# Starting the channel mixer's first product before its norm is known, in a two-layer decoder trunk on one core

## The chip, the cores and the metric

The kernel runs on one core of one Trainium2 chip, in one launch. Its time is device time in microseconds. Five engines work side by side, each through its own instructions in a fixed order: TensorE (PE in the profile, with its weight loads as PEld) multiplies, ScalarE (ACT) evaluates a function with a scale and a bias, VectorE (DVE) does elementwise work, GpSimd (POOL) here only raises to a power, and SyncE (SP) issues the loads. Engines meet at semaphores: an instruction waits until what it reads is written and what it overwrites has been read.

## What is computed

A trunk of two layers over 256 tokens of width 1024, all in float32. Each layer has a token mixer (three branches, gates, an output projection) and a channel mixer, each behind a norm whose shift and scale come from a conditioning vector c. The part that the change touches:

```python
def rms_norm(x, g):
    y = x * lax.rsqrt(jnp.mean(x * x, axis=-1, keepdims=True) + NORM_EPS)
    return y * g

def modulate(h, shift, scale):
    return h * (1.0 + scale[:, None, :]) + shift[:, None, :]

def channel_mixer(h, w_up, ffn_dw_w, ffn_dw_b, w_down):      # w_up: 1024 x 5632, w_down: 2816 x 1024
    u = causal_depthwise_conv(h @ w_up, ffn_dw_w, ffn_dw_b)  # 3 taps along the tokens
    a, b = jnp.split(u, 2, axis=-1)
    return (jax.nn.silu(a) * b) @ w_down

# in each layer, behind y = token_mixer(...) = merged @ w_out
x = x + g1[:, None, :] * y
h = modulate(rms_norm(x, ffn_norm_g[l]), sh2, sc2)
x = x + g2[:, None, :] * channel_mixer(h, w_up[l], ffn_dw_w[l], ffn_dw_b[l], w_down[l])
```

The norm's factor, called rstd below, is one number per token. So h @ w_up is rstd times (x * g * (1 + scale)) @ w_up, plus shift @ w_up, which is the same for all tokens.

## The kernel before

x lies transposed in SBUF, the on-chip memory: eight tiles of 128 features by 256 tokens (S). A product accumulates in PSUM, in banks of 512 float32 per partition, taken from two pools, psa and psb.

**Products.** Every float32 weight and every operand is split into a rounded high part and the low part that remains, and each product is three matmuls: high by high (L300), high weight by low operand (L301), low weight by high operand (L303). `mmw` queues products and `flush` issues them, all L303 behind all others; at the end of an accumulation it goes bank by bank instead (L294 to L296). A unit of weights is 128 x 1024, 512 KB: SP loads it into one of four `raw` buffers (L199), ACT writes its high part `whi` (L222), DVE its low part `wlo` (L224), which frees the buffer. `take` keeps some units split ahead of use; `issue_after` tells the scheduler to put an instruction behind another. The order on each engine is fixed when the program is built, by a scheduler that weighs these hints with estimates of its own.

**The boundary**, from the token mixer's projection to the channel mixer, lies in `layer` from L1249 on. `project(7)` ends the accumulation in four psa banks. Eight residuals (L1251) add it, times g1, to x. `norm_stats` then squares the eight tiles on ACT (L530), adds them in pairs on DVE (L540), and sums over the features in four pairs of one-column matmuls against a vector of ones (L545). DVE and POOL make rstd of that (L519, L520). `bcast_rows` spreads it over the partitions with a matmul against the identity (L555). Around these stand fourteen warm-up matmuls on a constant bf16 tile (L322, in groups of 4, 7 and 3 by `WARM1`), and filling steps: `mod_part(l, 5)` computes the last part of c's modulation, eight steps of four matmuls (L407) whose weights (`in_wm`) go through four spare buffers (`SPARE`). `norm_tile` makes the operand tile by tile: x times gain times rstd (L603, DVE), plus shift, rounded (L604, ACT), and the low part (L605, DVE). Then four small operations prepare the taps of the convolution.

**The channel mixer** runs 22 units up(j), each two weight units of four k-tiles with an a and a b half in one psb bank, and 22 units down(j), which accumulate in four psa banks. `FFN` orders them with `FLEAD` up units ahead of the downs. Behind up(j) come the taps on ACT (L1298) and DVE (L1300), silu and product, and the split of the result. In layer 0, the rows of layer 1's modulation (`in_wmr`, into spare buffers) fill DVE and SP.

## Time and profile before

| | us |
|---|---|
| three runs | 909.5, 912.25, 909.32 (median 909.5) |
| profiled execution | 909.82 |
| its span, first to last instruction | 907.7 |
| layer 0's boundary, projection's end to up(1)'s end | 271.13 to 291.76 |
| layer 1's boundary | 711.45 to 731.67 |
| layer 1's entry, sums of squares to broadcast's end | 464.62 to 469.04 |

The profile is of one execution. Its page gives busy times, the chain of work that ended last, and groups of instructions by line; the timeline lists each instruction with its start, and in brackets how long its engine had idled and who released it. A row such as `psa<-mhl,whi` names the output and the inputs by the program's names. The granted clock of TensorE (PEclk) is given as a share of full speed.

### The profile page before, as it was taken

The numbers are of one execution on the slowest core, as the hardware profiler recorded it, in microseconds if no ns is written. First come the engines' busy times: TensorE is split into PE (matmuls) and PEld (weight loads), VectorE is DVE, ScalarE is ACT, GpSimd is POOL, SyncE is SP. The second block draws the span as 40 slices with busy tenths as digits, with TensorE's granted clock in tenths as the row PEclk, the third lists the DMA queues.
The fourth block names the chain that finished last, engine by engine and source line by source line (L and its number), as shares of the span: only waits on it lengthen the run. The fifth ranks groups of instructions, "written<-read, shape, count | busy, mean of one in ns | idle before, by whom it ended". The sixth has DMA issues, their size and how long they took to land.

```text
span 907.7 us, 18736 instructions
## 1 busy us (share of the span) xinstructions
PE 888.3 (98%) x7339; PEld 841.5 (93%) x7339; DVE 797.1 (88%) x1554; ACT 555.2 (61%) x979; POOL 46.2 (5%) x36
## 2 busy tenths in 40 slices
PE   7999999999999999999999999999999999999998
PEld 6888888999998999999989988989999899999998
DVE  6989999999988999998764999999887798777774
ACT  4677588644755655556543676986475565565551
POOL 1010700000000000000000043000000000000000
PEclk9999999999999999999999999999999999999999
DMA  8956535699988889996633664157768676566631
GB/s 321 379 196 202 187 118 183 214 334 320 304 292 308 295 296 312 313 301 211 200 112 108 197 223 161 53 184 244 264 206 270 221 259 189 186 194 199 190 92 47
DMA packets 57976, 201.59 MB, mean 222 GB/s; under 512 B 6944, under 2 KB 8480, under 8 KB 57888
## 3 DMA queue, kind: packets, MB, share of 16 engines
q1 hardware_dynamic: 57888, 200.41, 66.6%
q8 instruction: 57, 0.93, 0.4%
q14 instruction: 31, 0.25, 0.1%
HBM read 199.33 MB, written 1.05 MB: 221 GB/s over the span
## 4 chain that ended last, share of the span: by engine, by line
PE 78%; DVE 12%; ACT 4%; DMA 3%; issue 2%; SPq 0%; POOL 0%; POOLq 0%; DVEq 0%; ACTq 0%
PE psb L300 16%; PE psb L301 16%; PE psb L303 15%; PE psa L300 7%; PE psa L301 7%; PE psa L303 7%; DVE wlo L224 3%; DVE cacc L1103 3%; PE psa L407 2%; DVE raw L778 1%; ACT whi L222 1%; PE psa L294 1%; DVE raw L390 1%; DMA raw<-in_win 1%; ACT p L675 1%
## 5 line engine op out<-in xcount | busy, mean ns | idle before, releaser
L222 ACT ACTIVATE whi<-raw 128x1024 fp32r<-128x1024 f32 (+2 forms) x286 | 296.6, 1043 | 217.6 <-PE psb L301 117.3
L224 DVE TENSOR_TENSOR wlo<-raw,whi 128x1024 fp32r<-128x1024 f32 (+2 forms) x286 | 340.3, 1195 | 65.5 <-ACT whi L222 57.9
L300 PE MATMUL psb<-hh,whi 128*128 128x256 f32 x1088 | 263.5, 282 | 0.5 <-ACT p L675 0.3
L301 PE MATMUL psb<-hl,whi 128*128 128x256 f32 x1088 | 261.0, 280 | 0.0
L300 PEld LDWEIGHTS psb<-hh,whi 128*128 128x128 f32 x1088 | 205.0, 189 | 6.3 <-issue 3.8
L301 PEld LDWEIGHTS psb<-hl,whi 128*128 128x128 f32 x1088 | 205.0, 189 | 0.5 <-DVE wlo L224 0.4
L303 PE MATMUL psb<-hh,wlo 128*128 128x256 f32 x1088 | 149.2, 279 | 0.0
L303 PEld LDWEIGHTS psb<-hh,wlo 128*128 128x128 f32 x1088 | 135.6, 188 | 0.8 <-issue 0.8
L1103 DVE SCALAR_TENSOR_TENSOR cacc<-upad,cw,cacc 128x256 f32<-128x256 f32 x240 | 105.7, 477 | 0.4
L300 PE MATMUL psa<-mhl,whi 128*128 128x256 f32 x400 | 94.0, 278 | 0.0
L301 PE MATMUL psa<-mhl,whi 128*128 128x256 f32 x400 | 93.7, 278 | 0.0
L1300 DVE SCALAR_TENSOR_TENSOR e<-psb,fw,e 128x255 f32<-128x255 f32 (+1 forms) x176 | 84.0, 477 | 5.4 <-ACT e L1298 4.5
L520 POOL TENSOR_TENSOR rs<-rs,mhalf 128x8 f32<-128x8 f32 (+3 forms) x26 | 44.6, 1729 | 669.2 <-DVE rs L519 669.1
L300 PEld LDWEIGHTS psa<-mhl,whi 128*128 128x128 f32 x400 | 75.0, 188 | 0.0
L301 PEld LDWEIGHTS psa<-mhl,whi 128*128 128x128 f32 x400 | 75.0, 188 | 0.0
L1298 ACT ACTIVATE e<-psb,fb,fw 128x256 f32<-128x256 f32 x88 | 48.5, 551 | 22.4 <-DVE e L1300 19.2
L390 DVE SCALAR_TENSOR_TENSOR raw<-raw,crow 128x1024 f32<-128x1024 f32 x48 | 58.5, 1218 | 0.5 <-DMA raw<-in_wmr 0.5
L303 PE MATMUL psa<-mhl,wlo 128*128 128x256 f32 x400 | 53.9, 277 | 0.0
L303 PEld LDWEIGHTS psa<-mhl,wlo 128*128 128x128 f32 x400 | 49.4, 188 | 0.0
L1308 ACT ACTIVATE mhl<-e 128x256 fp32r<-128x256 f32 x44 | 18.3, 416 | 30.1 <-DVE e L1306 27.6
L300 PE MATMUL psb<-whi,hh 128*128 128x416 f32 (+1 forms) x96 | 30.9, 350 | 4.5 <-ACT hh L854 4.5
L301 PE MATMUL psb<-whi,hl 128*128 128x416 f32 (+1 forms) x96 | 29.6, 343 | 0.2 <-DVE hl L855 0.2
(275 smaller groups left out, 1474.3 us busy)
## 6 DMA issues: line engine op xcount, KB each, us to landing
raw<-in_wup SPq DMA_DIRECT2D x88, 512.0 KB, 4.9
raw<-in_wmr SPq DMA_DIRECT2D x60, 512.0 KB, 5.7
raw<-in_wdn SPq DMA_DIRECT2D x44, 512.0 KB, 4.5
raw<-in_wm SPq DMA_DIRECT2D x32, 512.0 KB, 4.7
raw<-in_wgab SPq DMA_DIRECT2D x32, 512.0 KB, 4.9
raw<-in_wqkv SPq DMA_DIRECT2D x24, 512.0 KB, 5.1
raw<-in_win SPq DMA_DIRECT2D x16, 512.0 KB, 4.7
raw<-in_wgc SPq DMA_DIRECT2D x16, 512.0 KB, 4.3
```

What stands on the lines that cost most here:

```text
L222: ac.activation(hi, raw, AF.Copy)
L224: ve.tensor_tensor(lo, raw, hi.bitcast(F32), op=ALU.subtract)
L300: te.matmul(o, p1[0], p1[1], start=start, stop=False)
L301: te.matmul(o, p2[0], p2[1], start=False, stop=False)
L303: te.matmul(o, p3[0], p3[1], start=False, stop=stop)
L390: ve.scalar_tensor_tensor(raw, raw, scale, row, op0=ALU.mult, op1=ALU.mult, accum_out=acc)
L407: te.matmul(acc[32 * c:32 * c + 32, 0:S], cact[:, k:k + 1].to_broadcast([P, 32]), raw[:, c * S:(c + 1) * S], start=(k == 0), stop=(k == KD ...
L520: gp.tensor_tensor(r, r, mhalf[:, :n], op=ALU.pow)
L1103: ve.scalar_tensor_tensor(aj, upad[:, j, t:t + S], cw[:, j * 31 + t:j * 31 + t + 1], aj, op0=ALU.mult, op1=ALU.add)
L1298: ac.activation(t, src, AF.Identity, scale=fw[:, 2, c:c + 1], bias=fb[:, c:c + 1])
L1300: ve.scalar_tensor_tensor(t[:, d:S], src[:, 0:S - d], fw[:, 2 - d, c:c + 1], t[:, d:S], op0=ALU.mult, op1=ALU.add)
L1308: ac.activation(mh, th, AF.Copy)
```

## The change

Layer by layer, up(0) is taken apart from the other up units. Its operand becomes u = x * gain (without rstd and shift), split into high and low, and it starts as soon as the tiles of x are there. Two columns that hold the shift stand beside the 256 tokens of each operand tile, so that one matmul of 258 columns also gives shift @ w_up. The product stands in two psa banks (`pre`) and is multiplied by rstd, with the shift's column added, when it is read. The other up units still read the normalised tiles.

```diff
+    def raw_operand(sh):
+        parts = [operand([P, 4 * S], t, "u") for t in SPARE] + [
+            wk.tile([P, 4 * (S + 30)], F32R, tag="upad", name=nm("u"), bufs=1)]
...
+    def boundary(update, gs, sh, fill, part):
+        uh, ul = raw_operand(sh)
+        st = psb()
+        for n in range(KD):
+            update(n)
+            sq = e1()
+            ac.activation(sq, x[:, n, :], AF.Square)
+            if n % 2 == 0:
+                one = sq
+            else:
+                ve.tensor_tensor(one, one, sq, op=ALU.add)
+                if n < KD - 1:
+                    for b in range(NB):
+                        te.matmul(st[:, b:b + 1], one[:, b * P:(b + 1) * P], ones, start=(n == 1 and b == 0),
+                                  stop=False)
+            ac.activation(uh[n][:, 0:S], x[:, n, :], AF.Identity, scale=gs[:, n:n + 1])
+            ve.scalar_tensor_tensor(ul[n][:, 0:S], x[:, n, :], gs[:, n:n + 1], uh[n][:, 0:S].bitcast(F32),
+                                    op0=ALU.mult, op1=ALU.subtract)
+        mid = part(0, uh, ul)
+        with tc.issue_after(mid.ins):
+            for b in range(NB):
+                last = te.matmul(st[:, b:b + 1], one[:, b * P:(b + 1) * P], ones, start=False, stop=(b == 1))
+        r = rstd_of(st[:, 0:NB], NB, 1.0 / D)
+        with tc.issue_after(last.ins):
+            mid = part(1, uh, ul)
+        with tc.issue_after(mid.ins):
+            step(fill, 2)
+        with tc.issue_after(fills[-1].ins):
+            bc = bcast_rows(r)
+        with tc.issue_after(rows_last[0].ins):
+            step(fill, KD - 2)
+        return bc
...
+        def part0(part, uh, ul):
+            if part == 0:
+                pre.extend(psa() for _ in range(2))
+            behind[0] = 2
+            holds[:] = [rst[0].ins] if part else []
+            for k, w in take()[0]:
+                for i in range(2):
+                    mmw(pre[i][:, 0:S + 2], cut(w, i, P), (uh[k], ul[k]), k == 0, k == KD - 1)
+            return flush()
...
-        fill = mod_part(l, 5)
-        bc = norm_stats(fill)
+        fill = mod_part(l, 5, (("vb", 1), ("lh2", 1), ("lh0", 1), ("lh1", 1), ("qkT", 2), ("qkT", 2)))
+        bc = boundary(residual, gs2, mod[l][:, 24:32], fill, part0)
...
         def up(j):
-            pp = psb()
...
+            if j == 0:
+                bcs = e1()
+                ac.activation(bcs, bc, AF.Copy)
...
+                    ve.tensor_tensor(src, pre[i][:, 0:S], bcs, op=ALU.mult)
+                    cb = small(1, "m0", 4)
+                    ve.tensor_copy(cb, pre[i][:, S:S + 1])
+                    ac.activation(src, src, AF.Identity, bias=cb)
```

The order around it is changed too. The broadcast is a transpose in all norms, and no longer a float32 product; the warm-up matmuls of these two boundaries are gone (those of layer 1's entry stay). The filling weights have six buffers. `behind` lets `take` load units that it does not split yet, and `holds` names the instruction behind which the next low part is put:

```diff
-            rows_last[0] = te.matmul(bc[:, b * P:(b + 1) * P], r[:, b:b + 1].to_broadcast([P, P]), ident,
-                                     start=True, stop=True)
+            rows_last[0] = te.transpose(bc[:, b * P:(b + 1) * P], r[:, b:b + 1].to_broadcast([P, P]), ident)
...
-        while coming and len(ready) < n + ahead[0]:
+        while coming and len(ready) + len(raws_in) < n + ahead[0]:
             src, ks, lead = coming.pop()
-            ready.append((split(wload_unit(src), lead), src.shape[1] // len(ks), ks))
+            raws_in.append((wload_unit(src), lead, src.shape[1] // len(ks), ks))
+            while raws_in and len(ready) < n + ahead[0] - behind[0]:
+                raw, lead, c, ks = raws_in.pop(0)
+                ready.append((split(raw, lead), c, ks))
...
-FLEAD = 1
+FLEAD = 0
```

`behind` is 1 from project(6) on, 2 in up(0), and 0 behind it. The taps of the convolution are prepared earlier in the layer; the normalised tiles are each held behind the one two before; layer 1's tables (`prepare`, three kinds of small DVE operations) come to stand inside layer 0's boundary; `FLEAD` at 0 puts one more up unit ahead of down(0).

What the scheduler makes of it on PE, at layer 0's boundary, from the projection's end on. Before (psa_3532 is the filling accumulation, psb_3546 the sums of squares, psb_3589 the broadcast, psb_3671 up(0)):

```order
L407 MATMUL psa_3532<-raw_3533,cact 32x256 x4
L407 MATMUL psa_3532<-raw_3539,cact 32x256 x4
L545 MATMUL psb_3546<-ones,e_628_3547 128x1 x2
L545 MATMUL psb_3546<-ones,e_630_3554 128x1 x2
L322 LDWEIGHTS warm_w
L322 MATMUL psb_3545<-warm_w 128x256
...
L555 MATMUL psb_3589<-ident,rs_3586 128x128 x2
...
L407 MATMUL psa_3532<-raw_3595,cact 32x256 x4
L407 MATMUL psa_3532<-raw_3601,cact 32x256 x4
L407 MATMUL psa_3532<-raw_3607,cact 32x256 x4
L407 MATMUL psa_3532<-raw_3613,cact 32x256 x4
L300 MATMUL psb_3671<-hh_3631,whi_3376 128x256
```

After, from the low weights of up(0)'s first half (psa_3588 and psa_3589 are its two banks, psb_3537 the sums, psb_3664 the broadcast; the operand tiles u_3526 and u_3527 hold high parts, u_3529 low ones):

```order
L308 MATMUL psa_3588<-u_3527,wlo_3383 128x258
L308 MATMUL psa_3589<-u_3527,wlo_3383 128x258
L648 MATMUL psb_3537<-ones,e_633_3565 128x1 x2
L656 MATMUL psb_3537<-ones,e_635_3578 128x1 x2
L305 MATMUL psa_3588<-u_3527,whi_3462 128x258
L306 MATMUL psa_3588<-u_3529,whi_3462 128x258
...
L308 MATMUL psa_3589<-u_3530,wlo_3463 128x258
L413 MATMUL psa_3651<-raw_3652,cact 32x256 x4
L413 MATMUL psa_3651<-raw_3658,cact 32x256 x4
L560 MATMUL psb_3664<-ident,rs_3618 128x128 x2
L413 MATMUL psa_3651<-raw_3667,cact 32x256 x4
L413 MATMUL psa_3651<-raw_3673,cact 32x256 x4
```

Up(0) now stands ahead of the last sums and the broadcast, in two halves, and the filling steps stand behind it.

ACT in layer 0, from the projection's last operands (`mhl`, high part) to the first squares. Before:

```order
L222 ACTIVATE whi_3376<-raw_3374 128x1024
L1184 ACTIVATE mhl_3397<-e_604_3393 128x256
L1180 ACTIVATE e_609_3418<-psb_3405,col_146 128x256
L222 ACTIVATE whi_3456<-raw_3454 128x1024
L1184 ACTIVATE mhl_3422<-e_609_3418 128x256
L530 ACTIVATE e_628_3547<-x 128x256
L530 ACTIVATE e_629_3549<-x 128x256
L530 ACTIVATE e_630_3554<-x 128x256
L530 ACTIVATE e_631_3556<-x 128x256
```

After (raw_3590 is the second unit of up(1), the fourth up unit that SP loads; L641 are the squares, L650 the scaled x):

```order
L222 ACTIVATE whi_3382<-raw_3380 128x1024
L1245 ACTIVATE mhl_3403<-e_606_3399 128x256
L1241 ACTIVATE e_611_3424<-psb_3411,col_146 128x256
L222 ACTIVATE whi_3767<-raw_3590 128x1024
L222 ACTIVATE whi_3462<-raw_3460 128x1024
L1245 ACTIVATE mhl_3428<-e_611_3424 128x256
L641 ACTIVATE e_629_3539<-x 128x256
L650 ACTIVATE u_3526<-x,gs_3524 128x256
...
L650 ACTIVATE u_3527<-x,gs_3524 128x256
L222 ACTIVATE whi_3623<-raw_3466 128x1024
L222 ACTIVATE whi_3771<-raw_3621 128x1024
L641 ACTIVATE e_633_3565<-x 128x256
```

A split of raw_3590 has come between the two operands of the projection, and two splits stand between the fourth and the fifth tile.

ACT in layer 1, at the same place, after the change (raw_9431 is the fifth up unit that SP loads in this layer):

```order
L222 ACTIVATE whi_9224<-raw_9222 128x1024
L1245 ACTIVATE mhl_9210<-e_1569_9206 128x256
L222 ACTIVATE whi_9278<-raw_9276 128x1024
L222 ACTIVATE whi_9581<-raw_9431 128x1024
L641 ACTIVATE e_1590_9349<-x 128x256
L650 ACTIVATE u_9336<-x,gs_9334 128x256
...
L650 ACTIVATE u_9337<-x,gs_9334 128x256
L222 ACTIVATE whi_9433<-raw_9282 128x1024
L641 ACTIVATE e_1595_9380<-x 128x256
```

Here the added split stands behind the projection's last operand (mhl_9210) and right ahead of the first square, where before the squares followed the split of the unit loaded before it.

More of the change, by code (lines that the diff above doesn't have):

```diff
@@ L207, in trunk_kernel @@
     hold = [None]
+    holds = []
     raw_tags = [("raw", 4)]
@@ L222, in split @@
         ac.activation(hi, raw, AF.Copy)
-        with tc.issue_after(hold[0]) if hold[0] else ExitStack():
+        after = holds.pop(0) if holds else hold[0]
+        with tc.issue_after(after) if after else ExitStack():
             ve.tensor_tensor(lo, raw, hi.bitcast(F32), op=ALU.subtract)
@@ L302, in flush @@
         for o, _, _, p3, _, stop in queue:
-            te.matmul(o, p3[0], p3[1], start=False, stop=stop)
+            last = te.matmul(o, p3[0], p3[1], start=False, stop=stop)
         queue.clear()
+        return last
     def cut(w, i, n):
@@ L530, in sq_sums @@
             ac.activation(sq, src, AF.Square)
-            if alone and k >= n - 2:
-                one = sq
-            elif k % 2 == 0:
+            if k % 2 == 0:
                 if SQ4 and n == 4 and k:
@@ L542, in sq_sums @@
                     continue
-            with tc.issue_after(warm(bank, WARM1[0]).ins) if bank is not None and WARM1[0] and k == n - 2 + (not alone) else ExitStack():
+            with tc.issue_after(warm(bank, WARM1[0]).ins) if bank is not None and WARM1[0] and k == n - 1 else ExitStack():
                 for b in range(NB):
@@ L574, in norm_stats @@
             with tc.issue_after(last.ins):
-                step(fill, 3 if SHORT else KD - F1)
+                step(fill, KD - F1)
         return bc
@@ L606, in norm_tile, with ends @@
         return a, v
+    def raw_operand(sh):
+        uh, ul = [], []
+        parts = [operand([P, 4 * S], t, "u") for t in SPARE] + [
+            wk.tile([P, 4 * (S + 30)], F32R, tag="upad", name=nm("u"), bufs=1)]
+        for dst, (i0, i1), at in ((uh, (0, 1), 0), (ul, (2, 3), 2)):
+            for k in range(KD):
+                i, o = ((i0, i1, 4)[k // 3], k % 3 + (at if k > 5 else 0))
+                dst.append(parts[i][:, o * (S + 2):(o + 1) * (S + 2)])
+        for k0, k1 in ((0, 3), (3, 6), (6, 8)):
+            i, o = ((0, 1, 4)[k0 // 3], 0)
+            n = k1 - k0
+            def ends(i, o):
+                return parts[i][:, o * (S + 2):(o + n) * (S + 2)].rearrange("p (k c) -> p k c", k=n)[:, :, S:S + 2]
+            hi, lo = ends((0, 1, 4)[k0 // 3], 0), ends((2, 3, 4)[k0 // 3], 2 if k0 > 5 else 0)
+            src = sh[:, k0:k1].unsqueeze(2).to_broadcast([P, n, 2])
+            ac.activation(hi, src, AF.Copy)
+            ve.tensor_tensor(lo, src, hi.bitcast(F32), op=ALU.subtract)
+        return uh, ul
@@ L915, in layer @@
         upad = wk.tile([P, 4, S + 30], F32, tag="upad", name=nm("upad"), bufs=1)
-        ve.memset(upad[:, :, 0:30], 0.0)
+        with tc.issue_after(normed[0].ins) if l else ExitStack():
+            ve.memset(upad[:, :, 0:30], 0.0)
         def glu(j):
@@ L1267, in layer, with residual @@
             ve.tensor_scalar(fb[:, NF:44], cv(l, "fdw_b")[:, NF:44], 0.5, None, op0=ALU.mult)
+        for tok in CFG["order"][l]:
+            run[tok[0]](*tok[1:])
+            if tok == ("OC", 0):
+                taps()
+        step(mods, 99)
+        g1h = small(8, "g1h", 2)
+        ve.tensor_scalar(g1h, mod[l][:, 16:24], 0.5, None, op0=ALU.mult)
+        def residual(n):
+            ve.scalar_tensor_tensor(x[:, n, :], acc[n // 2][:, (n % 2) * S:(n % 2 + 1) * S], g1h[:, n:n + 1],
+                                    x[:, n, :], op0=ALU.mult, op1=ALU.add)
+        pre = []
+        def part0(part, uh, ul):
[7 more added lines that the diff above has]
+            return flush()
+        gs2 = mod_gain(l, 4, "ffn_g")
+        fill = mod_part(l, 5, (("vb", 1), ("lh2", 1), ("lh0", 1), ("lh1", 1), ("qkT", 2), ("qkT", 2)))
+        bc = boundary(residual, gs2, mod[l][:, 24:32], fill, part0)
+        hh, hl = new_h()
+        marks = []
+        for k in range(KD):
+            marks.append(norm_tile(k, bc, gs2[:, k:k + 1], mod[l][:, 24 + k:25 + k], hh, hl,
+                                   marks[k - 2] if k > 1 else None))
+        behind[0] = 0
         acc2 = []
@@ L1285, in up @@
         def up(j):
-            pp = psb()
-            for _ in range(2):
-                for k, w in take()[0]:
-                    for i in range(2):
-                        mmw(pp[:, i * S:(i + 1) * S], cut(w, i, P), (hh[:, k, :], hl[:, k, :]), k == 0 and i == 0,
-                            k == KD - 1 and i == 1)
-                flush()
+            if j == 0:
+                bcs = e1()
+                ac.activation(bcs, bc, AF.Copy)
+            else:
+                pp = psb()
+                for _ in range(2):
+                    for k, w in take()[0]:
+                        for i in range(2):
+                            mmw(pp[:, i * S:(i + 1) * S], cut(w, i, P), (hh[:, k, :], hl[:, k, :]), k == 0 and i == 0,
+                                k == KD - 1 and i == 1)
+                    flush()
             ab = []
```

58 lines of the change are left out of this document (26 added, 32 removed).

## Prediction

> **What bounds the kernel now.** First the head of the profile page: the span, the busy shares, and the engines of the chain of work that ended last.
>
> ```profile
> span 907.7 us, 18736 instructions
> PE 888.3 (98%) x7339; PEld 841.5 (93%) x7339; DVE 797.1 (88%) x1554; ACT 555.2 (61%) x979; POOL 46.2 (5%) x36
> PE 78%; DVE 12%; ACT 4%; DMA 3%; issue 2%; SPq 0%; POOL 0%; POOLq 0%; DVEq 0%; ACTq 0%
> ```
>
> TensorE (PE) is busy for 98% of the span, so the time falls only where PE does needless work or waits. The change works at the two boundaries between token mixer and channel mixer. PE's timeline at layer 0's boundary follows (start, duration, what ran; a row may hold several instructions, and a float32 product is recorded twice, so x16 at L407 is two steps of four).
>
> ```profile
> 271.13 1.07 PE L407 MATMUL psa<-raw,cact 128*32 128x256 f32 x16
> 272.13 1.05 PE L545 MATMUL psb<-ones,e 128*128 128x1 f32 x8
> 273.04 0.60 PE L322 MATMUL psb<-warm_w 128*128 128x256 bf16 x4
> 273.63 1.24 PE L545 MATMUL psb<-ones,e 128*128 128x1 f32 x8
> 274.74 0.92 PE L322 MATMUL psb<-warm_w 128*128 128x256 bf16 x7
> 275.97 0.71 PE L555 MATMUL psb<-ident,rs 128*128 128x128 f32 x4 [0.31 <-POOL rs L520]
> 276.52 0.49 PE L322 MATMUL psb<-warm_w 128*128 128x256 bf16 x3
> 276.94 1.93 PE L407 MATMUL psa<-raw,cact 128*32 128x256 f32 x32
> ...
> 281.19 0.64 PE L407 MATMUL psa<-raw,cact 128*32 128x256 f32 x8 [0.23 <-DMA raw<-in_wm]
> ...
> 290.86 1.07 PE L303 MATMUL psb<-hh,wlo 128*128 128x256 f32 x8
> 291.76 0.28 PE L300 MATMUL psb<-hh,whi 128*128 128x256 f32 x1
> 291.88 0.28 PE L301 MATMUL psb<-hl,whi 128*128 128x256 f32 x1
> ```
>
> The projection ends at 271.13, where the first filling step (L407) starts, and up(1) at 291.76: 20.6 us. Work that stays: up(0) and up(1), 96 matmuls at 0.1125 us (eight in the 0.90 from 290.86) to 0.12 (291.76 to 291.88), I take 0.116, 11.1 us; eight filling steps at 0.5 (two in the 1.00 from 271.13), 4.0; the sums of squares 0.91 and 1.11; the broadcast 0.55. Together 17.7, so **2.9 us are spare**: 14 warm-up matmuls (0.59, 0.92 and 0.42), the wait for rstd, 0.31, that for a load, 0.23, and short waits for normalised tiles. Layer 1:
>
> ```profile
> 711.45 1.07 PE L407 MATMUL psa<-raw,cact 128*32 128x256 f32 x16
> ...
> 730.77 1.07 PE L303 MATMUL psb<-hh,wlo 128*128 128x256 f32 x8
> ```
>
> From 711.45 to 731.67 (730.77 plus 0.90) are 20.2 us, 2.5 spare. **The ceiling at the two boundaries is 5.4 us, 0.6%**, if PE never waits there.
>
> **The change, part by part.** *The new chain that feeds PE.* PE begins up(0) without rstd, but needs its operand: for each of eight tiles ScalarE (ACT) makes a square and the rounded scaled x, VectorE (DVE) the residual and the remainder. ACT works in order:
>
> ```profile
> 264.40 1.07 ACT L222 ACTIVATE whi<-raw 128x1024 fp32r<-128x1024 f32 x1 [0.49 <-PE psa L301]
> 265.67 0.42 ACT L1184 ACTIVATE mhl<-e 128x256 fp32r<-128x256 f32 x1 [0.20 <-DVE e L1182]
> 271.46 1.01 ACT L530 ACTIVATE e<-x 128x256 f32<-128x256 f32 x3
> 290.11 0.57 ACT L1298 ACTIVATE e<-psb,fb,fw 128x256 f32<-128x256 f32 x1 [2.18 <-DVE e L1300]
> 290.57 0.41 ACT L1304 ACTIVATE e<-e 128x256 f32<-128x256 f32 x1
> ```
>
> A square costs 0.32 us (three in 1.01, less the overlap), an activation whose scale is a column, as that of scaled x is, 0.46 (290.11 to 290.57), a weight split 0.96 (1.07 less an overlap of 0.1). In layer 0 two splits stand between the fourth and the fifth tile: 8 x 0.78 + 2 x 0.96 = **8.2 us** from the first square to the last scaled tile, against 4.3 of PE's own (24 matmuls, three pairs of sums at 0.5). ACT is late here, not PE.
>
> *When this chain starts in layer 0.* In the new order ACT does one more split, of raw_3590, ahead of the high half of the projection's last operand (row 265.67 before). That unit is the fourth up unit that SP loads, issued at 261.4 in the trace of before:
>
> ```profile
> L199 SPq DMA_DIRECT2D raw<-in_wup x1: 328/328/328, 261.4 to 261.4; - x1
> DMA to landing us min/median/max: 5.4/5.4/5.4
> ```
>
> ```profile
> 265.11 0.28 PE L294 MATMUL psa<-mhl,whi 128*128 128x256 f32 x1
> 266.14 0.50 PE L294 MATMUL psa<-mhl,whi 128*128 128x256 f32 x2 [0.19 <-ACT mhl L1184]
> ```
>
> The load's issue hangs on a buffer whose release does not move, so it lands at 261.4 + 5.4 = 266.8 as before. ACT stands until then; two splits and the operand follow, to 266.8 + 1.92 + 0.3 = 269.0. PE, in its last flush of the projection since 265.11, has 11 matmuls (1.25 us) that don't need it, and stands from 266.4 to 269.0: **2.6 us**, where it waited 0.19 before. Sixteen matmuls later the first bank is whole; with drain and residual,
>
> ```profile
> 268.06 1.66 DVE L1251 SCALAR_TENSOR_TENSOR x<-psa,g1h,x 128x256 f32<-128x256 f32 x4 [0.95 <-PE psa L296]
> 271.64 1.22 DVE L224 TENSOR_TENSOR wlo<-raw,whi 128x1024 fp32r<-128x1024 f32 x1
> ```
>
> the first residual (268.06 before, 0.40 each) comes at 271.0 and the first square at 271.4. The fourth tile is ready at 274.9, ten more matmuls end at 276.1, and PE stands again, but for one pair of sums, until the last square's sum at 279.6. Then 0.6 for that sum, the second half of up(0) 2.8, and 10.0 of filling steps (4.0), broadcast (0.35) and up(1) (5.6): 293.0 against 291.76, **+1.2 us**. Had the load landed in 3 us, nothing would stand at 266.4 and the same sum gives -0.6.
>
> *The filling weights.* Six buffers in place of four remove the 0.23 us at 281.19. But the last two loads now stand on SP behind four others, three of which wait for the tiles that up(0) reads; so they leave at about 284 in a queue of five loads and are needed at 288. I take +0.5, of 0 to 2.0.
>
> *Layer 1.* Here the late split stands behind the projection's operands, straight ahead of the first square. Its unit, raw_9431, takes the buffer, and so the place, of the load issued at 704.9:
>
> ```profile
> L199 SPq DMA_DIRECT2D raw<-in_wup x1: 327/327/327, 704.9 to 704.9; - x1
> DMA to landing us min/median/max: 4.6/4.6/4.6
> ```
>
> ```profile
> 708.01 0.81 ACT L530 ACTIVATE e<-x 128x256 f32<-128x256 f32 x2 [1.69 <-DVE x L1251]
> ```
>
> Landed at 709.5, split at 710.45: the first square moves from 708.01 to 710.45. With one split among the tiles, 8 x 0.78 + 0.96 = 7.2: last scaled tile at 717.65, the last sums in PE done at 718.25, then 2.8 and 10.0: 731.0 against 731.67, **-0.7 us**. PE idles 2.0 us in pieces, most of it from 715.2 on.
>
> *The broadcast as a transpose*, at the boundaries (counted above) and at layer 1's entry:
>
> ```profile
> 468.04 1.21 PE L555 MATMUL psb<-ident,rs 128*128 128x128 f32 x4 [0.33 <-POOL rs L520]
> 298.91 0.44 PE L415 MATMUL psa<-ident,e 128*128 128x128 f32 x2
> ```
>
> Two transposes take 0.44, two float32 products 0.71 to 1.21: -0.3 at the entry, of 0 to -0.7.
>
> *What is added beside other work.* DVE has eight remainders more (0.40 each), and for up(0) two products with rstd and two copies (1.0 together); all eight tiles are still normalised. It was full in this stage already (columns: PE, its weight loads, DVE, ACT, POOL busy, then granted clock, DMA share, GB/s):
>
> ```profile
> 276.94:291.90 14.96, 14.73 (x147) 12.64 (x147) 14.96 (x31) 11.29 (x18) 0.00 (x0) 1.00 0.85 291
> ```
>
> After the broadcast DVE has 16 operations of 0.40 and the low half of the second unit (1.13: 271.64's row less the overlap) ahead of the last normalised tile, 7.5 us; PE has four filling steps and most of up(1). They tie, so I count nothing and keep 0 to +1.0 a boundary. Two more columns of 256 are 48 x 0.001 us, nothing; an operand that ran at half rate for its odd stride would cost 48 x 0.12 = 5.8 a boundary, yet all 256-column rows stand 0.11 to 0.12 apart, so I take nothing. One more up unit ahead of down(0) is the same work: 0.
>
> *The clock.* The warm-up matmuls go. What their lack may do shows at layer 1's entry, where the last three rows are windows of PE (length, busy, granted clock, DMA share, GB/s):
>
> ```profile
> 465.98 0.60 PE L322 MATMUL psb<-warm_w 128*128 128x256 bf16 x4
> 466.78 0.93 PE L322 MATMUL psb<-warm_w 128*128 128x256 bf16 x7
> 468.00:468.25 0.25, 0.21 (x1) 0.68 1.10 366
> 471.25:471.50 0.25, 0.25 (x8) 0.50 0.00 0
> 471.50:471.75 0.25, 0.25 (x12) 1.00 0.00 0
> ```
>
> The clock was at half from about 468.08 to 471.5, 3.4 us. In the 3.4 before, PE had only these 11 wide matmuls, 1.2 us without drain; the rest were one-column sums and a wait. At 273.5 to 276.9 in layer 0, 0.92 + 0.55 + 0.42 = 1.9 us were wide, and the clock stayed. So about a third of wide work in such a stretch loses the clock, and half keeps it. In the new layer 0 the 4.1 us from 276.1 to 280.2 have no wide work: nearly every position of a 3.4 us stretch (9 in 10) falls under a third. Half clock for 3.4 us costs 1.7 less what is idle in it: **+1.3 us**. In layer 1 the empty stretch is 3.0 us, and I give it evens.
>
> The Trainium skill, "TensorE: Matmul & The Clock Gate", section "What's actually happening", has the clock fall after an idle window of about 3.4 us, without a share of wide work. The sums of squares break this idleness, so by that rule nothing falls and the sum below is 1.3 us lower. The drop at 468.08 after a stretch that was busy but sparse speaks against so strict a reading.
>
> **Sum.** Layer 0: +1.2, +0.5 and +1.3. Layer 1: -0.7 with the clock kept. Its entry: -0.3. Together +2.0. The profiled execution took 909.8 us for a span of 907.7, 0.3 above the median of the three runs; reckoned from that median, 909.5, the forecast is **911.5 us**, and so are the rivals.
>
> **Rivals.**
>
> - *Slower beyond doubt: the clock falls at layer 1 too, or at the stall in the projection, or the filling weights land at their late bound.* One mechanism, ACT ahead of PE holding it for 2 us and more; it decides where under a third of 3.4 us is wide. Each adds 1.3 to 1.5: 912.9 to 914.4. Chance 0.30.
> - *The clock stays.* Only the waits are left: +0.7, 910.2. For it: the sums of squares in the gap; against: 468.08. Chance 0.14. The skill's rule above is of this kind.
> - *The loads land early.* For it: nothing else has to move, and the shortest such load of the trace would do; against: those here took 5.4 and 4.6. Then layer 0 gives -0.6 and layer 1 -1.8, the entry -0.3, with the drop -1.4 (908.1), without it -2.7 (906.8), with no wait at all -5.7 (903.8). Chance 0.18.
> - *DVE is the bound behind the boundary:* +1.0 at each on the forecast, 913.5. Chance 0.06.
> - *The change doesn't take rstd off the path:* the new order has the last sums, part one of up(0) and two filling steps between; rstd needed 1.1 (274.87 to 275.97) and gets 3.8. Excluded.
>
> **How the numbers follow.** The forecast (one drop, 910.5 to 912.2) has 0.32. About 0.3%, 2.7 us, is what a measurement of this kernel tells from no change. Slower by more: the first and the fourth rival and the edge of the forecast, 0.38. Faster by more: the better half of the third, 0.10. The same: 0.52. The range leaves out the best of the early loads and the first rival with two of its prices: 907.0 to 914.5.
>
> **What would show it.** In layer 0 a wait of PE of 2 to 3 us inside the projection's last flush, released by ACT's high half, while ACT waits for a DMA; a second wait of some 3.5 us in two pieces between the halves of up(0), released by DVE or ACT; then a granted clock of half for 3.4 us. In layer 1 ACT waiting for a DMA until 709.5 of this clock ahead of the first square. The forecast fails if ACT finds its unit there, if the granted clock stays at one, if the 258-column matmuls stand over 0.12 us apart, or if PE waits for a normalised tile in up(1).

## The result, and the profile after

| | before | after |
|---|---|---|
| median of the runs, us | 910.98 (15 runs, 906.64 to 918.80) | 919.65 (15 runs, 912.78 to 926.70) |
| ratio, 95% interval | | **1.0084 [1.0058, 1.0109]** |
| profiled execution, us | 909.82 | 920.29 |
| mean granted clock | 0.9957 (the 29 runs beside e1) | 0.9916 (15 runs) |

The changed kernel is slower by 0.84%, some 7.7 us (8.7 between the medians, 10.4 between the two profiled executions), where 2.0 were forecast. The time lies outside the range that was given. The head of the page after, with the span, the busy time of each engine and the engines of the chain that ended last:

```profile
span 918.1 us, 18670 instructions
PE 888.3 (97%) x7299; PEld 841.4 (92%) x7299; DVE 803.7 (88%) x1584; ACT 562.1 (61%) x1007; POOL 47.9 (5%) x36
PE 68%; DVE 15%; DMA 7%; ACT 6%; issue 3%; SPq 1%; POOL 0%; DVEq 0%; ACTq 0%; POOLq 0%
```

PE's busy time is the same 888.3 us in a span that is 10.4 longer. PE holds 68% of the chain, where it held 78%, and DMA, DVE and ACT take the rest. So the change took a little work from PE (the warm-up matmuls) and put waits in its place. Stage by stage, by the end of PE's last matmul of each stage in the two timelines:

| stage | before | after | difference | forecast |
|---|---|---|---|---|
| start to the end of up(1), layer 0 | 291.76 | 296.16 | +4.4 | +3.0 |
| from there to the last down unit, layer 0 | 171.7 | 177.0 | **+5.3** | 0 |
| layer 1's entry and token mixer | 247.8 | 246.7 | -1.2 | -0.3 |
| layer 1's boundary and channel mixer | 192.2 | 194.1 | +1.9 | -0.7 |

Before loses its clock for 3.4 us in the third of these stages, after at the end of the second (see below): up to 1.7 us of the +5.3 and most of the -1.2 are this one shift.

PE's timeline after, its waits at both boundaries and at the end of layer 0's channel mixer (the bracket is the wait and who ended it):

```profile
269.29 0.39 PE L299 MATMUL psa<-mhl,whi 128*128 128x256 f32 x1 [2.01 <-ACT mhl L1245]
...
279.39 0.61 PE L648 MATMUL psb<-ones,e 128*128 128x1 f32 x4 [0.16 <-DVE e L645]
280.80 0.61 PE L656 MATMUL psb<-ones,e 128*128 128x1 f32 x4 [0.81 <-DVE e L645]
...
285.36 0.43 PE L560 MATMUL psb<-ident,rs 128*128 128x128 f32 x2
...
291.55 0.64 PE L413 MATMUL psa<-raw,cact 128*32 128x256 f32 x8 [0.43 <-DMA raw<-in_wm]
...
306.13 0.44 PE L422 MATMUL psa<-ident,e 128*128 128x128 f32 x2 [1.05 <-ACT e L419]
...
461.44 0.39 PE L300 MATMUL psa<-mhl,whi 128*128 128x256 f32 x1 [0.64 <-DVE mhl L1403]
...
466.72 0.62 PE L299 MATMUL psa<-mhl,whi 128*128 128x256 f32 x3 [2.31 <-ACT mhl L1402]
...
751.76 0.44 PE L422 MATMUL psa<-ident,e 128*128 128x128 f32 x2 [1.34 <-ACT e L419]
```

The first wait is the one forecast inside the projection's last flush. The rstd is no longer waited for: the broadcast at 285.36 has no bracket. The waits at 306.13, 461.44, 466.72 and 751.76 stand behind the boundary, where the forecast has nothing. ACT's timeline shows how the first wait comes about, and the front of both boundaries:

```profile
266.93 2.00 ACT L222 ACTIVATE whi<-raw 128x1024 fp32r<-128x1024 f32 x2 [2.43 <-DMA raw<-in_wup]
268.84 0.40 ACT L1245 ACTIVATE mhl<-e 128x256 fp32r<-128x256 f32 x1
272.94 0.42 ACT L641 ACTIVATE e<-x 128x256 f32<-128x256 f32 x1 [3.69 <-DVE x L1327]
...
280.10 0.50 ACT L650 ACTIVATE u<-x,gs 128x256 fp32r<-128x256 f32 x1
...
717.69 1.06 ACT L222 ACTIVATE whi<-raw 128x1024 fp32r<-128x1024 f32 x1 [2.79 <-DMA raw<-in_wup]
718.65 0.40 ACT L641 ACTIVATE e<-x 128x256 f32<-128x256 f32 x1
```

ACT stood 2.43 us for the load until 266.93 and split two units before the operand that PE needed. In layer 1 it stood 2.79 us, straight ahead of the first square. Windows of PE (length, busy, granted clock, DMA share, GB/s) give the clock:

```profile
266.70:270.10 3.40, 1.39 (x12) 1.00 0.96 381
270.00:270.25 0.25, 0.25 (x4) 0.79 1.04 410
273.50:273.75 0.25, 0.25 (x4) 0.88 0.24 98
468.00:468.25 0.25, 0.25 (x4) 0.74 0.57 229
471.50:471.75 0.25, 0.25 (x4) 0.93 0.00 0
```

The clock fell at 270.15 (0.79 is 58% of a quarter at full and the rest at half) and at 468.12, each time for 3.4 us and each time behind a wait of 2 us and more. Before, it fell once behind its start, at layer 1's entry; at the start both kernels have such a stretch, from 10.7 to 14.1. Last, windows of DVE (length, busy, then clock, DMA share, GB/s), after and then before:

```profile
280.00:300.00 20.00, 15.51 (x32) 1.00 0.85 295
...
320.00:340.00 20.00, 17.56 (x34) 1.00 0.73 244
340.00:360.00 20.00, 16.64 (x28) 1.00 0.81 259
...
440.00:460.00 20.00, 19.83 (x37) 1.00 0.73 229
```

```profile
280.00:300.00 20.00, 18.84 (x36) 1.00 0.92 326
...
320.00:340.00 20.00, 19.79 (x39) 1.00 0.87 298
340.00:360.00 20.00, 20.00 (x39) 1.00 0.90 308
...
440.00:460.00 20.00, 14.93 (x27) 1.00 0.62 193
```

Over these three early windows DVE stood 10.3 us idle after, and 1.4 before. It has more to do, and it catches up only at the end: before, it has 5 us to spare at 440 to 460; after, it has none, and PE waits for it.

What the two engines waited for from 280 to 360 stands in the lists of waits (total, times, longest): ACT after, ACT before, and DVE after.

```profile
ACT whi L222 <- DMA raw<-in_wup: 16.3, 13, 3.7
ACT whi L222 <- DMA raw<-in_wdn: 4.8, 4, 1.6
```

```profile
ACT whi L222 <- DMA raw<-in_wup: 1.5, 1, 1.5
```

```profile
DVE e L1394 <- ACT e L1392: 4.8, 4, 2.2
DVE e L606 <- PE psb L560: 3.1, 1, 3.1
```

ACT stands 21.1 us for weight units in this stretch, where it stood 1.5 before, and the taps that DVE needs (L1392) stand behind these splits: at 341.64 a split had waited 2.42 us, its tap followed at 342.61, and DVE had waited 2.15 us for it. So the mechanism of the first wait, a split that waits for its load ahead of other work of ACT, goes on far behind the boundary. Why the loads come late there was not tested.

### The profile page after: what moved, and what is told of

It reads as the page before. It is cut to its first block, busy times and chain, and to the rows that moved or that the text cites. A ratio compares the mean times of both kernels' runs of the same rounds, so it can differ in the third digit from the quotient of the medians.

```text
span 918.1 us, 18670 instructions
## 1 busy us (share of the span) xinstructions
PE 888.3 (97%) x7299; PEld 841.4 (92%) x7299; DVE 803.7 (88%) x1584; ACT 562.1 (61%) x1007; POOL 47.9 (5%) x36
## 3 DMA queue, kind: packets, MB, share of 16 engines
HBM read 199.33 MB, written 1.05 MB: 218 GB/s over the span
## 4 chain that ended last, share of the span: by engine, by line
PE 68%; DVE 15%; DMA 7%; ACT 6%; issue 3%; SPq 1%; POOL 0%; DVEq 0%; ACTq 0%; POOLq 0%
PE psb L305 13%; PE psb L306 13%; PE psb L308 13%; PE psa L305 7%; PE psa L306 7%; PE psa L308 7%; DVE wlo L225 5%; DVE cacc L1164 3%; DMA raw<-in_wup 2%; ACT whi L222 2%; PE psa L413 1%; DVE raw L838 1%; DMA col<-in_cols 1%; DVE raw L396 1%; DMA raw<-in_win 1%
## 5 line engine op out<-in xcount | busy, mean ns | idle before, releaser
L305 PE MATMUL psb<-hh,whi 128*128 128x256 f32 x1056 | 256.5, 283 | 0.5 <-ACT p L735 0.3
L306 PE MATMUL psb<-hl,whi 128*128 128x256 f32 x1056 | 253.6, 280 | 0.0
L305 PEld LDWEIGHTS psb<-hh,whi 128*128 128x128 f32 x1056 | 198.9, 188 | 6.1 <-issue 3.0
L306 PEld LDWEIGHTS psb<-hl,whi 128*128 128x128 f32 x1056 | 198.9, 188 | 0.9 <-DVE hl L608 0.8
L308 PE MATMUL psb<-hh,wlo 128*128 128x256 f32 x1056 | 145.2, 279 | 0.3 <-DVE wlo L225 0.3
L308 PEld LDWEIGHTS psb<-hh,wlo 128*128 128x128 f32 x1056 | 131.7, 188 | 1.3 <-issue 0.8
L1394 DVE SCALAR_TENSOR_TENSOR e<-psb,fw,e 128x255 f32<-128x255 f32 (+1 forms) x168 | 80.2, 478 | 12.6 <-ACT e L1392 11.8
L1392 ACT ACTIVATE e<-psb,fb,fw 128x256 f32<-128x256 f32 x84 | 46.5, 553 | 32.4 <-DVE e L1394 29.1
```

Of the source, the lines that this page charges most:

```text
L305: te.matmul(o, p1[0], p1[1], start=start, stop=False)
L306: te.matmul(o, p2[0], p2[1], start=False, stop=False)
L308: last = te.matmul(o, p3[0], p3[1], start=False, stop=stop)
L1392: ac.activation(t, src, AF.Identity, scale=fw[:, 2, c:c + 1], bias=fb[:, c:c + 1])
L1394: ve.scalar_tensor_tensor(t[:, d:S], src[:, 0:S - d], fw[:, 2 - d, c:c + 1], t[:, d:S], op0=ALU.mult, op1=ALU.add)
```

## The experiments

Theory A is that of the prediction: ACT's early weight splits hold PE, and the waits lose the clock. Rival B: DVE falls behind and holds the end of the channel mixer. Rival C: the loads of the filling weights and of layer 1's rows are in each other's way. Rival D: the missing warm-up matmuls are the loss. Each edit is on the kernel named; ratios are against the kernel before.

**e1, on after: the high splits are held behind the last scaled tile.**

```diff
-        ac.activation(hi, raw, AF.Copy)
+        with tc.issue_after(hi_hold[0]) if hi_hold[0] else ExitStack():
+            ac.activation(hi, raw, AF.Copy)
...
+        hi_hold[0] = scaled.ins
```

> The changed kernel, with the high-part splits of up(1) held on ACT behind the last scaled tile, so that none stands ahead of the projection's last operand (layer 0) or of the first square (layer 1). Theory A (ACT standing for a late load is the start of the loss): PE's wait of 2.0 us at the high half of the last operand falls to about 0.2, the half clock from 270 to 273.5 goes (1.7), one split less stands among the tiles (0.5 to 1.0): 4 us below the changed kernel, about 915.5. Rival B (DVE runs late through the whole channel mixer of layer 0, so what is won ahead of it is given back at its end): the early wait goes, the waits at the end of layer 0's channel mixer (3.2 us) grow by as much, and the time stays within 1 us of the changed kernel.

Measured: 914.16 us, 1.0065 [1.0034, 1.0095]. PE's wait at the projection's last operand went from 2.01 to 0.19, and the sums' from 0.97 to 0.29. But PE's timeline and the SP queue's show a new wait:

```profile
286.88 0.64 PE L415 MATMUL psa<-raw,cact 128*32 128x256 f32 x8 [1.91 <-DMA raw<-in_wm]
```

```profile
274.42 4.08 SPq L198 DMA_DIRECT2D raw<-in_wmr  x3
278.61 0.37 SPq L198 DMA_DIRECT2D raw<-in_wup  x1
280.72 0.80 SPq L198 DMA_DIRECT2D raw<-in_wm  x2
```

The last two filling weights leave behind three rows and a unit, land 6.6 us later (the median in the list of loads), and hold PE for 1.91 us. So A is right about its wait, and C is what stands behind it: of 2.5 us that are freed, 1.5 come back (the 1.91 less the 0.43 of after). In time the gain on after is not clear of the noise, as the two intervals overlap; 4 us were expected.

**e2, on after: the eight gate rows of layer 1 are taken out** (the bias alone is copied, so their product with c is left out).

```diff
-                mod_row(crow1[0], l, 2, k, scale=0.5 if CDMA else 1.0)
+                ve.tensor_copy(mod[l][:, 16 + k:17 + k], modb[:, l, 16 + k:17 + k])
```

> The changed kernel, with 8 of the 24 modulation rows that DVE works off during layer 0's channel mixer replaced by a copy of their bias (their loads and products with c are left out). Theory B (DVE is late there by what it could not do early): PE's 3.2 us of waits for the last down units of layer 0 go to 0 and the kernel is 3 to 4 us below the changed one, about 916. Rival C (the waits there come from the order of the last units, whatever DVE did before): they stay above 2 us, and the time stays within 1 us of the changed kernel. The early wait of 2.0 us stays under both.

Measured: 914.54 us, 1.0061 [1.0034, 1.0088]. In the last 30 us of layer 0's channel mixer PE has no wait left, where after has 3.2 us; the early wait stays (2.11). That is what B expects: less work for DVE, and the wait is gone. But this trace alone does not show it. It is of an execution of 924.82 us, whose matmuls also stand farther apart behind 340 (87 in the 10 us from 400, where after has 91), so PE itself came later to the end. The gain in time on after is not clear of the noise either. e6 and e8 are the cleaner test.

**e3, on after: the four transposes of the modulation move two units back** (`if j == 1: step(fill)` becomes `j == 3`), since they waited 1.05 and 1.34 us for ACT's copy.

> The changed kernel, with the end of the filling product (copy, two transposes, sum) put behind up(3) in place of up(1). Theory D (the two transposes stand on PE ahead of ACT's copy): the waits of 1.05 us in layer 0 and 1.34 in layer 1 go and the kernel gains 2.4 us. Rival: PE only waits elsewhere for the same late ACT and DVE, and the gain is under 1 us.

Measured: 918.41 us, 1.0108 [1.0068, 1.0148]: nothing is won. The transposes do not wait, but PE's and DVE's timelines show who does:

```profile
311.00 0.55 PE L305 MATMUL psb<-hh,whi 128*128 128x256 f32 x1 [2.77 <-DVE mod L397]
```

```profile
309.20 0.42 DVE L1403 TENSOR_TENSOR mhl<-e,mhl 128x256 fp32r<-128x256 f32 x1 [1.28 <-ACT mhl L1402]
```

The same lag appears one step later, and longer, and the clock falls there (at 310.94). The wait belonged to the lag of ACT and DVE, not to the transposes. At the end of layer 0's channel mixer PE then waits 0.17 us, where after has 3.2, though DVE has all its work: PE, held up earlier, no longer comes before DVE is ready.

**e4, on before: the warm-up matmuls of the two boundaries are taken out** (`WARM1[:] = (0, 0, 0)` ahead of `norm_stats`, and back behind it).

> The kernel before, without the fourteen warm-up matmuls at each of the two boundaries (those at layer 1's entry stay). Theory W1 (they only cost their time): 3.9 us less PE work, of which the wait for rstd takes back 2 x 1.0, so 907 to 909. Theory W2 (they hold the clock): half clock for 3.4 us at one or both boundaries, plus 1.7 each, so 909 to 912 and a granted clock of 0.994 or less.

Measured: 910.0 us, 1.0000 [0.9972, 1.0029]. D falls. Windows of PE in its trace:

```profile
275.75:276.00 0.25, 0.25 (x2) 0.54 0.98 393
279.00:279.25 0.25, 0.25 (x6) 0.64 0.71 180
716.00:716.25 0.25, 0.25 (x4) 0.67 0.77 311
```

Without the warm-up matmuls the clock falls at both boundaries, at 275.77 and 716.09. They take 1.9 us of PE at each boundary, 3.9 in all, and without them as much is lost elsewhere: 1.4 us by the mean clock of the runs (0.9942 against 0.9957), 1.4 us by longer waits for the sums and for rstd at the two boundaries, and 1.29 us by a wait for the transposes behind layer 0's (the waits are of this trace). Of the 5.4 us that the prediction called the ceiling, 3.9 were therefore never to be had by removing them alone.

**e5, on before: only the broadcast becomes a transpose** (`te.transpose` in place of the product with the identity).

> The kernel before with one part of the change alone: the broadcast as a transpose. If only its PE time counts, 0.2 to 0.5 us less at layer 1's entry and at each boundary, 0.6 to 1.0 in all (908.5 to 909); rival: rstd and the filling steps hide it at the boundaries and the time stays within 0.3 us. Both are below what the timing can tell; the rows of the profile tell.

Measured: 907.89 us, 0.9997 [0.9977, 1.0017]. It is too small to tell from nothing, as the -0.3 us of the forecast.

**e6, on e1: the eight gate rows move behind the last normalised tile of layer 1's entry.**

```diff
-                mod_row(crow1[0], l, 2, k, scale=0.5 if CDMA else 1.0)
...
+        if l > 0:
+            for k in range(KD):
+                with tc.issue_after(normed[0].ins):
+                    mod_row(crow1[0], l, 2, k, scale=0.5 if CDMA else 1.0)
```

> The changed kernel with the splits held (as in e1) and the eight rows of layer 1's gate moved from layer 0's channel mixer to behind the last normalised tile at layer 1's entry (all is computed). If the two causes add (theory A: 2.2 us by the early wait; theory B: 3 us by DVE's lag), the waits at the end of layer 0's channel mixer go to under 0.3 us and the kernel stands 5 to 6 us below the changed one, ratio to before about 1.003. Rival: DVE's work only moves into layer 1, where PE then waits for it, and the ratio stays at e1's 1.0065.

Measured: 914.21 us, 1.0073 [1.0054, 1.0093], no better than e1. The list of PE's waits at the end of layer 0's channel mixer, after and then e6 (total, times, longest):

```profile
PE psa L299 <- ACT mhl L1402: 2.5, 2, 2.3
PE psa L300 <- DVE mhl L1403: 0.6, 1, 0.6
```

```profile
PE psa L301 <- ACT mhl L1408: 0.2, 1, 0.2
```

B's wait is gone there without any work left out: e1, which differs in the rows alone, still waits 2.39 us at that place. But layer 1's entry and token mixer now take 250.9 us against 246.7 of after (up to 1.7 of that is a stretch at half clock, which fell here), and the filling weights' waits stay (1.58 and 0.64). The rows cost about as much in the next stage as they had cost in this one.

**e7, on e1: the filling weights get eight buffers in place of six.**

```diff
-(("vb", 1), ("lh2", 1), ("lh0", 1), ("lh1", 1), ("qkT", 2), ("qkT", 2))
+(("vb", 1), ("lh2", 1), ("lh0", 1), ("lh1", 1), ("qkT", 2), ("qkT", 2), ("kv", 2), ("thc", 1))
```

> The changed kernel with the splits held and eight buffers for the filling weights in place of six, so that the last two loads leave before the boundary. If the wait of 1.9 us for them, which e1 showed in layer 0 (and 0.4 in layer 1), stands on the path, it goes and the kernel gains 2 us on e1, ratio about 1.004 to 1.005. Rival (layer 0's channel mixer is bound by DVE anyway): the wait goes and the waits at its end grow by as much, ratio unchanged at 1.0065.

Measured: 910.03 us, 1.0016 [0.9999, 1.0033]. All waits for `in_wm` are gone, and with the splits held the two buffers are worth some 0.5% (1.0065 to 1.0016). That it is the late weights that cost so much is not shown: the waits that go are 2.3 us, and two more buffers gain 0.41% on the kernel before as well (e12), where PE waited 0.23 us for a load. In their place PE waits 1.05 and 0.52 us for normalised tiles of up(1) and 1.42 for the transposes, and the end of layer 0 still waits 2.42 us:

```profile
463.69 0.62 PE L301 MATMUL psa<-mhl,whi 128*128 128x256 f32 x3 [2.42 <-ACT mhl L1405]
```

**e8, e6 and e7 together.** All eight rows moved, the splits held, eight buffers.

> All three: splits held, rows moved, eight buffers. If the causes add, no wait above 0.5 us is left in layer 0 but that for the transposes, and the kernel comes to within 1 us of before, ratio 0.999 to 1.001, with a granted clock of 0.994 to 0.996. If the change could win at all (its ceiling of 5.4 us), it should show here: below 0.998. Rival: lost clock keeps it above 1.003.

Measured: 909.3 us, 1.0016 [0.9997, 1.0034]. The wait at layer 0's end is gone (0.16, where e7, which differs in the rows alone, has 2.42), but the token mixer of layer 1 has one of 2.11 us for DVE in its place. The ratio is e7's: no win of the change shows.

**e9, on e7: four of the eight rows moved**, four left where they were, so that neither stage has all of them.

> The changed kernel with the splits held, eight buffers for the filling weights, and four of the eight gate rows of layer 1 moved to its entry (e8 moved all eight and PE then waited 2.1 us there for DVE). If DVE's lag at layer 0's end (2.4 us in e7) and the crowding at layer 1's entry (2.1 us in e8) are both matters of a few rows, both waits fall under 0.5 us and the kernel is 2 us below before: ratio 0.997 to 0.999. Rival: one of the waits stays, ratio 1.000 to 1.002.

Measured: 904.34 us (5 runs), 0.9957 [0.9944, 0.9970], faster than the kernel before. e8 differs from it in the rows alone, and so where they stand is worth about 0.59%; PE's waits in the two traces account for part of that only. What is left at layer 0's boundary, in PE's and ACT's timelines:

```profile
288.41 0.50 PE L307 MATMUL psb<-hh,whi 128*128 128x256 f32 x2 [2.35 <-ACT hh L609]
```

```profile
286.90 1.06 ACT L224 ACTIVATE whi<-raw 128x1024 fp32r<-128x1024 f32 x1 [3.20 <-DMA raw<-in_wup]
```

ACT stands again before a weight split for a late load, now ahead of a normalised tile. It is the mechanism of the first wait at another place. From 280 to 360 ACT still stands 23.5 us for weight units.

**e10, on after: eight buffers alone**, with neither splits held nor rows moved.

> The changed kernel with eight buffers for the filling weights alone; the splits stand where the change put them. If the two causes add, it lies between the changed kernel (1.0084) and e7 (1.0016), at about 1.004 to 1.005: the early wait of 2.0 us and the clock that it costs stay, the waits for filling weights go. Rival (the held splits were what mattered, and the buffers only in their wake): no gain, 1.008.

Measured: 914.59 us (5 runs), 1.0060 [1.0046, 1.0073]. Alone it takes 0.24% off, as holding the splits alone takes 0.19%; both together (e7) take 0.68%. PE still waits 1.74 us at the projection's last operand, 1.51 for the sums and 2.57 at the end of layer 0. So one cure without the other does little; but with intervals of 0.15 to 0.3% on each, the 0.25% by which the pair beats the sum is likely, not shown.

**e11, on e9: `FLEAD` back to 1.**

> As e9, with the order of the first up and down units put back to that of before (one up unit fewer ahead of down(0)). If that order carries none of the time, the same ratio as e9 within 0.15%; if the additional up unit is what covers DVE's lag behind the boundary, down(0) waits for its operand and it is 1 us or more above e9.

Measured: 908.71 us, 1.0004 [0.9990, 1.0018]. The transposes wait 1.92 and 1.08 us. So the added up unit ahead of down(0), which was forecast at 0, is worth about 0.5% on that base. That it gives ACT and DVE room is a part of it, by these waits; of the 3.7 us between the two profiled executions the channel mixers hold only 0.7, and the rest is not traced.

**e12, on before: six buffers for the filling weights in place of four**, nothing else of the change.

```diff
-        fill = mod_part(l, 5)
+        fill = mod_part(l, 5, SPARE + ("kv", "thc"))
```

> The kernel before with two more buffers for the filling weights of its boundaries (six in place of four, the two of e7 to e11). If what e9 gains over before comes from the buffers alone (the wait of 0.23 to 0.48 us for a load, and the closer spacing of the matmuls behind the boundary, 0.113 in place of 0.118 us until up(8), 2 us a layer), this kernel gains 2 to 5 us too, ratio 0.995 to 0.998. If it comes from the change itself (up(0) ahead of the norm), the ratio stays at 0.999 to 1.001.

Measured: 906.03 us, **0.9959 [0.9940, 0.9977]**. The kernel before gains from more buffers as much as e9 does with everything. Of its 3.7 us, 1.6 go with the clock: the mean over its nine runs is 0.9973, over the runs of before beside it 0.9955.

**e13, e9 once more.**

> The kernel of e9 a second time, on another chip and beside e12 and e14. If its gain is real, the ratio is 0.994 to 0.998 again; if it was the luck of five runs, it comes out at e7's 1.0016 or near it.

Measured: 906.6 us, 0.9960 [0.9945, 0.9974]. One execution of the eight took 2244 us; it is not in the ratio, and its cause is not known. e9's gain is real, and the same as e12's.

**e14, on before: `PAIRS = (2, 5)` in place of `(2, 8)`**, which moves the up unit whose splits are placed with their own leads three units forward. It was to test what the gain of e12 is made of; the last section says how far it does.

> The kernel before, with the one pair of units whose weights are placed differently in their buffers (its offsets of 0 and 40 elements, where all others have 16) moved from up(8) to up(5). In the profile of before the matmuls stand 0.118 us apart from the boundary until up(8) and 0.113 behind it. If that pair sets the spacing of all that follows, the step moves to up(5), some 24 us earlier in each layer, and the kernel gains about 1 us a layer (ratio 0.998). If the step is set by something else, it stays near 346 and 785 us and the time stays.

Measured: 907.79 us, 0.9980 [0.9967, 0.9994], as the first reading expects.

## Why the prediction was wrong

**The wait in the projection's last flush: right.** The load landed at 266.93 (forecast 266.8), PE stood 2.01 us until 269.29 (2.6 until 269.0), released by ACT's high half. The wait is shorter because PE came to the flush later, at 265.82 and not at 265.11: its matmuls stand farther apart in the 20 us ahead of it (87 in the 10 us from 250, where before has 90). e1 removes the cause, and the wait is 0.19.

**ACT's chain: right in length, wrong in what followed.** From the first square to the last scaled tile it took 7.7 us (280.60 less 272.94) where 8.2 were forecast. The second stand, forecast at 3.5 us in two pieces, came to 0.97 us only. The clock fell already at 270.15, inside the flush. So PE itself came later to the place where it was to wait: by an estimate, 1.7 us at half clock and 0.7 by the later start, which is about the 2.5 us that it waited less. In the forecast the clock fell after the second stand. Up to the end of up(1) the terms +1.2, +0.5 and +1.3 make 3.0, and 4.4 was measured, so 1.4 us of the miss lie here; 0.7 of it is the later start of the flush.

**"They tie, so I count nothing": the step that failed.** It compared DVE's and PE's work between the broadcast and the last normalised tile, and went no further. DVE did lose little there. But it waited 3.1 us for the broadcast at its start, it waits 4.8 us for ACT's taps behind late loads, and it still has all of layer 1's rows to do in this stage, as before. It stays behind to the end of the channel mixer: PE waits there 3.2 us (0.22, 0.64 and 2.31) and 1.05 us at the transposes, and the 2.31 loses the clock a second time. These 4.2 us and the 1.7 of the lost clock more than make up the +5.3, where the forecast has 0. e6 against e1, and e8 against e7, differ in the rows alone, and with the rows out of this stage the wait at its end falls from 2.4 us to 0.16. So DVE's load is shown to make that wait; that the backlog begins with ACT's late loads is read from the trace and was not tested. The fourth rival had the right engine, at +1.0 a boundary and a chance of 0.06; it priced a tie within 15 us and not a backlog over 180.

**The filling weights: right in the sum, wrong as a bound.** They left at 285.06 (forecast "about 284") and cost 0.43 and 0.36 us in the changed kernel, near the +0.5, though this was booked for layer 0 alone. Yet they were a hidden second bound: with ACT's wait gone they hold PE for 1.91 us (e1), and with two more buffers not at all (e7).

**Layer 1: the front right, the rest missing.** Layer 1's boundary starts 8.6 us later after than before. Less these, ACT had its unit at 709.1 (forecast 709.5) and made the first square at 710.1 (710.45). The -0.7 then came to +1.9, for want of three terms: the wait for the filling weights, 0.36, that of an up unit for its low weights, 0.29, and that of the transposes, 1.34. These 2.0 us are most of the 2.6 us that separate forecast and measurement. The rest goes with matmuls that stand farther apart in this stage, not traced to one place.

**The clock: one stretch more, as forecast, but at other places, and too little.** One stretch at half clock was forecast between the halves of up(0), net of that at layer 1's entry, which both kernels were to have. Behind its start the profiled execution has two in place of one. That the number agrees is luck: they lie in the projection's flush, the place of the first rival, and at the end of layer 0's channel mixer, and none behind the second stand. Over its runs the mean clock is 0.9916 against 0.9957. A stretch of 3.41 us at half clock lowers the mean by 0.0019, so this is about two more stretches a run, and 0.0041 x 918 = 3.8 us of the 8.7 between the medians. The prediction booked 1.3. It asked at each place whether the clock falls; it is rather a chance at each place where PE waits about 2 us, and the changed kernel has more such places. Its rule, that a third of wide work in such a stretch loses the clock and a half keeps it, is not contradicted: PE was busy for 41% of the 3.41 us ahead of each of the two falls.

**Warm-up matmuls, transposed broadcast, 258 columns.** e4 and e5 bear on the first two: without the warm-up the kernel takes the same time, and the transpose cannot be told from nothing. The 258-column matmuls stand 0.12 us apart in the trace, as forecast. That the change frees rstd is true as well: no wait for it is left at either boundary, but there it had cost 0.31 and 0.30 us.

Together: the waits behind the boundary (4.2 us in layer 0, 2.0 in layer 1) and the clock that they and the first wait lose are the size of the miss. And the change has nothing to set against them. Repaired three ways (e9, e13) it runs at 0.996, and the kernel before with two more buffers (e12) at 0.9959: of starting up(0) before rstd nothing measurable is left. The runs of e12 had the higher clock, though (0.9973 against 0.9957 in e13), which is worth 1.5 us; a gain of that size is not excluded.

## What to carry to other kernels

Work that is moved to the front of a boundary can make the helpers behind it late. So follow their backlog to the end of the stage, where the last unit asks for it, and not to the next meeting point alone. A wait that is removed shows the next load in line, so price the second-latest input as well. And before the credit for a repaired change is booked, run its side edits (here two buffers) on the old kernel.

## What the chip showed unexpectedly

**The clock's windows lie on a grid.** One stretch at half clock lasts 3.41 us (270.15 to 273.56). In the trace after, the two falls lie 468.12 - 270.15 = 197.97 us apart, which is 58 such stretches of 3.413; in e4 716.09 - 275.77 = 440.32, 129 of them. So a wait should lose the clock only if enough of it falls in one cell of this grid: 2.01 us at 269.29 and 2.31 at 466.72 lost it in one run, while 2.42 us at 463.69 in e7 and 2.35 at 288.41 in e9 did not, in theirs. Reckoned on from the falls at the start of each run, the cell of each wait held 1.40 us of busy PE in both losses of after and 1.50 in the loss of e1 at 287.81, but 1.77 in e7 and 1.48 in e9, which kept the clock. As 1.50 lost it and 1.48 kept it, something else counts too; what it is stays open. This fits the spread of one kernel's runs: the changed kernel's mean clock is between 0.984 and 0.998. The Trainium skill, "TensorE: Matmul & The Clock Gate", section "What's actually happening", gives a free-running window of 3413 ns, and the traces agree to the figure. Its condition of an idle window they do not bear out: in the 3.4 us ahead of 270.1 PE was busy 1.39 us with twelve instructions.

**Matmuls of one shape keep two distances.** Windows of 10 us of PE, full in each, with the count of matmuls in brackets: first before (two windows), then after and e5. The last two are e9 and e13, which are the same kernel.

```profile
324.00:334.00 10.00, 10.00 (x87) 1.00 0.88 306
...
350.00:360.00 10.00, 10.00 (x91) 1.00 0.93 310
```

```profile
324.00:334.00 10.00, 10.00 (x88) 1.00 0.77 256
```

```profile
324.00:334.00 10.00, 10.00 (x91) 1.00 0.82 286
```

```profile
745.00:755.00 10.00, 10.00 (x91) 1.00 0.70 231
```

```profile
745.00:755.00 10.00, 10.00 (x88) 1.00 0.71 219
```

From start to start they stand 0.118 us apart in some stretches and 0.113 in others, at full clock, with the same shapes. In before the distance changes at about 346, behind the up unit that starts at 340.3, and in after at about 350. With six buffers in before (e12) it is 0.113 from 302 on, and with `PAIRS` moved by three units (e14) it changes behind the unit that starts at 317.4, three units earlier. 44 us at the wide distance are 44 x 4/91 = 1.9 us longer, so it is tempting to put the gains of both kernels down to it.

The runs do not bear that out. e9 and e13 run the same instructions in the same order on every engine, and in layer 1 they stand at different distances: the program alone does not set it, and one trace of a kernel does not tell what its other runs do. Nor does the distance order the times: e5's matmuls stand close in both layers and it measured 0.9997; e8's stand close and it measured 1.0016, as e7 did at the wide distance. What sets the distance stays open, and so does what e12 and e14 gain by.

In the change's own loss the wider distance has a small part: the 0.7 us by which after comes later to the projection's last flush, and some tenths in layer 1.
